# First stage of an encoder: x times rstd made ahead of the modulation for four half tiles, two of them reading the spread from PSUM

## The chip, the cores and the metric

The kernel runs on one core of one Trainium2 chip. The core has TensorE (PE, with its weight loads shown apart as PEld), VectorE (DVE), ScalarE (ACT), GpSimd (POOL) and SyncE (SP, which here issues the transfers). Each engine works through its own list of instructions in order, and waits at an instruction for what other engines or transfers must have done. The metric is the time of one execution on the device, in microseconds (us), lower is better.

## The reference

Two layers over 1024 tokens of 1024 channels. Each layer is conditioned by a vector c through a shift, a scale and a gate (adaLN); only the start of layer 0 matters here:

```python
def rms_norm(x, g):
    xf = x.astype(jnp.float32)
    y = xf * lax.rsqrt(jnp.mean(xf * xf, axis=-1, keepdims=True) + EPS)
    return (y * g.astype(jnp.float32)).astype(x.dtype)
...
    c_act = jax.nn.silu(c)
    for l in range(DEPTH):
        mod = c_act @ ada_w[l] + ada_b[l]
        shift, scale, gate = jnp.split(mod, 3, axis=-1)
        h = rms_norm(x, norm_g[l]) * (1.0 + scale[:, None, :]) + shift[:, None, :]
        if l % 2 == 0:
            y = even_mixer(h, ...)      # proj = h @ w_in, then attention and a recurrence
        else:
            y = odd_mixer(h, ...)       # proj = h @ w_in, then neighbourhood attention
        x = x + gate[:, None, :] * y
    return rms_norm(x, final_g)
```

So every element of h is x · rstd(token) · gain(channel) + shift(channel), where rstd is one over the root of a token's mean square, and gain is norm_g · (1 + scale). Layer 0's first projection multiplies h by w_in.

## The kernel before, in words

x is kept transposed: channels on the 128 partitions, tokens along the free axis. It is eight tiles of 128 channels by 1024 tokens (xT, tiles 0 to 7), and each has two halves of 512 tokens (half 0 and half 1). A pair of tiles, 2g and 2g+1, is a group g.

A product in fp32 quality is made from three products in a shorter format: high by high, high by low and low by high. Weights come as slabs of 128 output channels, 128x1024 with all eight tiles of input channels (raw). ScalarE rounds a slab to its high part (whi, L185), GpSimd subtracts to get its low part (wlo, L186). For the activations ScalarE writes the high part (ahi, L408) and VectorE the low one (alo, L409).

The first stage runs while x, the first slabs and the pieces of the adaLN weights (ada) are still coming in:

- `squares(hf, on_dve, ...)` loads the eight tiles of a half and squares them, some on VectorE (L528: tiles 2 and 5 in half 0; 1, 4 and 7 in half 1) and the others on ScalarE (L530). PE adds the squares up over the channels (L371, 32 matmuls of 128 columns for a half, of which the profile lists 64 passes, into a bank of PSUM named norm). In half 1 tile 7 is the first that is added, and the others follow it.
- `scale(hf)`: eleven small operations on VectorE make rstd of 512 tokens, folded to 128x128 (`rstd_rows`, L381 to L387), PE spreads it to all partitions (L400, into the same bank), and ScalarE copies that from PSUM to SBUF (bcs, L548).
- `mod_first(g)`: PE makes shift and scale of group g from ada and c (L276), ScalarE copies the row (mrow, L299), PE turns it into columns (L301), and VectorE makes shift (first, L305) and gain (L307).
- `parts(g, hf)` calls `make_h` for the two tiles: on VectorE x becomes x · gain · bcs (L407), ScalarE adds the shift for the high part (L408), VectorE makes the low part (L409). The tile is overwritten by x · rstd · gain, to which a later stage adds the shift again.
- `products(i, g, hf)`: the three products of slab i with each of the two tiles (L566, L567, L568), added up in PSUM banks, one for each of slabs 0, 1, 2 and half.

The kernel is written in a rough order, and a scheduler sets the order of each engine's list from that order, its estimates of times, and two marks: `tc.high_priority()` (the block is taken early) and `tc.issue_after(x)` (not before instruction x has been taken). The list of each engine is fixed when the kernel is built. SP's list of transfers is one of these.

Behind the first stage come the rest of layer 0's projections, differential attention, the recurrence, the output projection, and layer 1. They are not touched.

## Time and profile before

| | before |
|---|---|
| runs of the kernel, us | 1191.19, 1193.62, 1196.17 |
| median, us | 1193.62 |
| profiled execution, us | 1190.94 |
| its span in the profile, us | 1189.2 |
| mean granted clock of TensorE | 0.994 |
| share of the span busy: PE, PEld, DVE, ACT, POOL | 96%, 82%, 62%, 47%, 31% |

The span runs from the first to the last instruction that the profile has; the profiled execution's own time is 1.7 us longer. Rows of a timeline read: start in us, length in us (of the whole row, where several instructions follow each other as one row, xN), engine, line, operation, what it writes and reads, and in brackets how long the engine had been idle before it and who released it. A row of a group with three numbers in a line (476/482/2407) gives the shortest, the middle and the longest of its instructions in ns.

### The profile page before, as it was taken

Reading aid. Unit: us, or ns where it says so; the run is one execution under the profiler, and the core shown is the slowest. Engines: PE = TensorE matmul, PEld = TensorE weight load, DVE = VectorE, ACT = ScalarE, POOL = GpSimd, SP = SyncE. Lnnn points to the kernel's source line nnn. Section 1 sums busy time; section 2 is a strip of 40 time slices with the busy share of each in tenths; the row PEclk is TensorE's granted clock in tenths of the full one; section 3 lists DMA queues with packets and bytes.
Section 4 is the critical chain, followed back from the end, with each engine's and each line's share of the span. In section 5 each row is a group of like instructions: output and inputs, shape, how many; then the busy total and the mean of one; then the engine's idle time right before and its main releaser. Section 6 shows DMA issues by size and latency. Waiting matters only on the chain.

```text
span 1189.2 us, 19214 instructions
## 1 busy us (share of the span) xinstructions
PE 1142.0 (96%) x7232; PEld 972.3 (82%) x7232; DVE 735.6 (62%) x1422; ACT 564.4 (47%) x1029; POOL 372.5 (31%) x346
## 2 busy tenths in 40 slices
PE   4999899999998999999999999999999999999997
PEld 3788668888887888777878888988998998888896
DVE  6867948699889989768763334233434443556354
ACT  4358486465655556523443444344444434445121
POOL 2124321243333322344413333332333333326100
PEclk8999999999999999999999999999999999999999
DMA  9723132422123112476513442243453544314212
GB/s 331 234 87 117 53 96 74 141 74 82 37 79 88 32 39 72 136 245 225 181 53 121 136 116 83 87 141 101 131 171 96 152 133 120 90 38 161 92 72 71
DMA packets 85789, 136.46 MB, mean 115 GB/s; under 512 B 8000, under 2 KB 49472, under 8 KB 85696
## 3 DMA queue, kind: packets, MB, share of 16 engines
q1 hardware_dynamic: 85696, 135.23, 36.4%
q8 instruction: 57, 0.93, 0.3%
q14 instruction: 36, 0.29, 0.1%
HBM read 112.13 MB, written 16.78 MB: 108 GB/s over the span
## 4 chain that ended last, share of the span: by engine, by line
PE 75%; DVE 12%; ACT 5%; DMA 3%; issue 2%; POOL 2%; SPq 0%; DVEq 0%; ACTq 0%; POOLq 0%
PE pp L201 14%; PE pp L203 14%; PE pp L202 14%; PE no L1383 4%; PE etr L1365 3%; PE v L201 2%; PE v L203 2%; PE v L202 2%; PE n L662 2%; PE atr L998 2%; DVE e L968 2%; PE n L663 2%; PE s L662 1%; PE s L663 1%; POOL wlo L186 1%
## 5 line engine op out<-in xcount | busy, mean ns | idle before, releaser
L201 PE MATMUL pp<-ahi,whi 128*128 128x512 f32 (+1 forms) x976 | 370.2, 379 | 1.0 <-DVE sgb L668 0.9
L203 PE MATMUL pp<-ahi,wlo 128*128 128x512 f32 (+1 forms) x976 | 367.7, 377 | 1.1 <-POOL wlo L186 1.1
L202 PE MATMUL pp<-alo,whi 128*128 128x512 f32 (+1 forms) x976 | 368.0, 377 | 0.0
L186 POOL TENSOR_TENSOR wlo<-raw,whi 128x1024 fp32r<-128x1024 f32 x80 | 196.8, 2463 | 267.6 <-ACT whi L185 249.1
L203 PEld LDWEIGHTS pp<-ahi,wlo 128*128 128x128 f32 x976 | 183.8, 188 | 35.4 <-POOL wlo L186 1.6
L201 PEld LDWEIGHTS pp<-ahi,whi 128*128 128x128 f32 x976 | 183.8, 188 | 34.0 <-DVE sgb L668 1.7
L202 PEld LDWEIGHTS pp<-alo,whi 128*128 128x128 f32 x976 | 183.9, 188 | 30.4
L1354 POOL TENSOR_SCALAR e<-e,r 128x288 f32<-128x288 f32 (+1 forms) x128 | 71.5, 572 | 234.7 <-DVE r L1352 234.4
L185 ACT ACTIVATE whi<-raw 128x1024 fp32r<-128x1024 f32 x80 | 84.3, 1056 | 105.3 <-PE pp L202 57.4
L972 ACT ACTIVATE e<-e,nm 128x1024 f32<-128x1024 f32 x64 | 73.6, 1150 | 47.1 <-DVE nm L968 46.7
L1349 ACT ACTIVATE e<-e,nm 128x288 f32<-128x288 f32 (+1 forms) x128 | 72.7, 569 | 46.1 <-DVE nm L1346 39.3
L1371 DVE COPY e<-etr 96x384 f32<-96x384 f32 (+1 forms) x64 | 35.5, 555 | 94.3 <-PE etr L1365 92.7
L1346 DVE CUSTOM_DVE_ANT_0 e<-n,bias 128x288 f32<-128x288 f32 (+1 forms) x128 | 60.6, 505 | 46.9 <-PE n L663 32.9
L1369 ACT ACTIVATE e<-etr 96x384 f32<-96x384 f32 (+1 forms) x64 | 31.3, 490 | 118.2 <-DVE e L1371 116.7
L968 DVE CUSTOM_DVE_ANT_0 e<-s,tb 128x1024 f32<-128x1024 f32 x64 | 77.3, 1219 | 6.7 <-PE s L663 4.9
L989 POOL TENSOR_SCALAR e<-e,r 128x256 f32<-128x256 f32 x32 | 32.7, 1021 | 131.6 <-DVE r L978 81.4
L201 PE MATMUL v<-whi,ahi 128*128 128x256 f32 x256 | 72.2, 282 | 0.0
L203 PE MATMUL v<-whi,alo 128*128 128x256 f32 x256 | 71.9, 281 | 0.0
L202 PE MATMUL v<-wlo,ahi 128*128 128x256 f32 x256 | 71.9, 281 | 0.0
L1005 ACT ACTIVATE ath<-atr 128x512 fp32r<-128x512 f32 x64 | 37.5, 596 | 38.1 <-PE atr L998 37.8
L1365 PE MATMUL etr<-ident,e 128*96 128x128 f32 (+1 forms) x384 | 52.5, 272 | 2.0 <-POOL e L1354 2.0
L662 PE MATMUL s<-ks,qq 128*128 128x512 f32 x128 | 52.5, 410 | 0.4 <-DVE nm L968 0.4
(218 smaller groups left out, 2108.5 us busy)
## 6 DMA issues: line engine op xcount, KB each, us to landing
raw<-in_w_dram SPq DMA_DIRECT2D x56, 512.0 KB
ada<-in_adaw_dram SPq DMA_DIRECT2D x96, 256.0 KB
raw<-in_wo_dram SPq DMA_DIRECT2D x24, 512.0 KB
bias<-in_nab_dram SPq DMA_DIRECT2D x64, 144.0 KB
qq<-qq SPq DMA_DIRECT2D x48, 128.0 KB
bias<-in_nab_dram SPq DMA_DIRECT2D x32, 192.0 KB
xT<-in_xT_dram SPq DMA_DIRECT2D x16, 256.0 KB
vd<-vt SPq DMA_DIRECT2D x32, 128.0 KB
```

Of the source, the lines that this page charges most:

```text
L185: A.activation(hi[:], raw[:], AF.Copy)
L186: G.tensor_tensor(lo[:], raw[:], hi[:], ALU.subtract)
L201: T.matmul(ps, lh, rh, start=start, stop=False)
L202: T.matmul(ps, lh, rl, start=False, stop=False)
L203: state["pe"] = T.matmul(ps, ll, rh, start=False, stop=stop).ins
L662: T.matmul(dst, qsel(q[m]), k, start=True, stop=False)
L968: state["dve"] = V.tensor_tensor_reduce(out=e[:], in0=ps[:].rearrange("p a b -> p (a b)"), in1=tbt["tb"][:, o:o + S], scale=-1.0, scalar=3 ...
L972: A.activation(e[:], e[:], AF.Exp, scale=-1.0, bias=nm[:], accum_out=sums[:, m:m + 1])
L1346: state["dve"] = V.tensor_tensor_reduce(out=e[:, m, :n], in0=ps[:, m, :n], in1=bias["now"][m][:, :n], scale=-1.0, scalar=3.0e38, op0=ALU.a ...
L1349: A.activation(e[:, m, :n], e[:, m, :n], AF.Exp, scale=-1.0, bias=nm[:, m:m + 1], accum_out=sums[:, m:m + 1])
L1354: state["pool"] = G.tensor_scalar(e[:, m, :n], e[:, m, :n], r[:, m:m + 1], 0.0, ALU.mult, ALU.add).ins
L1365: T.transpose(pt[:kn, m, j * P:(j + 1) * P], e[:, m, j * kn:(j + 1) * kn], ident[:])
```

## The change

For tiles 0, 1, 2 and 3 of half 0 the product with rstd is an instruction of its own (`scale_x`, a TENSOR_TENSOR on VectorE), issued before the gain is known: for tiles 0 and 1 straight after the spread, reading it from its bank in PSUM (norm), for tiles 2 and 3 behind the low part of tile 1, reading bcs. `make_h` then, for these four, lets ScalarE multiply by the gain and add the shift in one instruction (a scale and a bias pointer), and after it VectorE multiplies the tile by the gain (TENSOR_SCALAR) and makes the low part as before. The other tiles of group 0 (0 and 1 in half 1) keep the fused product, and read norm where they read bcs.

```diff
-    def make_h(l, k, hf, x, bc):
+    def make_h(l, k, hf, x, bc, scaled=False):
...
-        V.scalar_tensor_tensor(x, x, g, bc, ALU.mult, ALU.mult)
-        A.activation(hi[:], x, AF.Identity, bias=b)
-        V.scalar_tensor_tensor(lo[:], x, b, hi[:], ALU.add, ALU.subtract)
+        if scaled:
+            A.activation(hi[:], x, AF.Identity, scale=g, bias=b)
+            V.tensor_scalar(x, x, g, None, ALU.mult)
+        else:
+            V.scalar_tensor_tensor(x, x, g, bc, ALU.mult, ALU.mult)
+            A.activation(hi[:], x, AF.Identity, bias=b)
+        state["lo"] = V.scalar_tensor_tensor(lo[:], x, b, hi[:], ALU.add, ALU.subtract).ins
         hact[k, hf] = (hi, lo)
...
+        scaled = set()
+
+        def scale_x(k, hf):
+
+            V.tensor_tensor(half(k, hf), half(k, hf), (bcs if k > 1 else nbank)[hf][:], ALU.mult)
+            scaled.add((k, hf))
+
         def parts(g, hf):
             for k in (2 * g, 2 * g + 1):
-                make_h(0, k, hf, half(k, hf), bcs[hf][:])
+
+                make_h(0, k, hf, half(k, hf), (bcs if g else nbank)[hf][:], (k, hf) in scaled)
...
         scale(0)
+        scale_x(0, 0)
+        scale_x(1, 0)
         parts(0, 0)
+        with tc.issue_after(state["lo"]):
+            scale_x(2, 0)
+            scale_x(3, 0)
```

In the changed kernel the lines shift: the multiplication is L558, the high part of a tile that is scaled already L408, its plain product L409, the fused product L411, the high part behind it L412, the low part L413, VectorE's square L532, ScalarE's L534, the copy of the spread L552. VectorE's list grows from 1395 to 1399 rows, the other lists keep their lengths. The lists of GpSimd and SP are the same as before; those of PE, VectorE and ScalarE differ within the first stage alone. In the rows below the numbers behind a name count buffers: xT_116 to xT_123 are tiles 0 to 7, ahi_0 and alo_0 belong to half 0, ahi_1 and alo_1 to half 1, raw_299 and raw_300 and so on to the slabs.

VectorE, from the end of rstd of half 0 to the first small operation for half 1, before:

```order
L305 TENSOR_TENSOR first_291<-mod_239,sm 128x4
L307 SCALAR_TENSOR_TENSOR gain_292<-first_291,sm 128x2
L407 SCALAR_TENSOR_TENSOR xT_116<-xT_116,gain_292,bcs 128x512
L407 SCALAR_TENSOR_TENSOR xT_117<-xT_117,gain_292,bcs 128x512
L409 SCALAR_TENSOR_TENSOR alo_0_322<-xT_116,first_291,ahi_0_321 128x512
L409 SCALAR_TENSOR_TENSOR alo_0_327<-xT_117,first_291,ahi_0_326 128x512
L528 TENSOR_TENSOR sq<-xT_117 128x512
L528 TENSOR_TENSOR sq<-xT_120 128x512
L528 TENSOR_TENSOR sq<-xT_123 128x512
L381 TENSOR_SCALAR rs<-norm_339 128x128
```

and in the changed kernel:

```order
L558 TENSOR_TENSOR xT_116<-xT_116,norm_190 128x512
L558 TENSOR_TENSOR xT_117<-xT_117,norm_190 128x512
L305 TENSOR_TENSOR first_291<-mod_239,sm 128x4
L307 SCALAR_TENSOR_TENSOR gain_292<-first_291,sm 128x2
L409 TENSOR_SCALAR xT_116<-xT_116,gain_292 128x512
L413 SCALAR_TENSOR_TENSOR alo_0_324<-xT_116,first_291,ahi_0_323 128x512
L532 TENSOR_TENSOR sq<-xT_117 128x512
L409 TENSOR_SCALAR xT_117<-xT_117,gain_292 128x512
L413 SCALAR_TENSOR_TENSOR alo_0_329<-xT_117,first_291,ahi_0_328 128x512
L558 TENSOR_TENSOR xT_118<-xT_118,bcs 128x512
L558 TENSOR_TENSOR xT_119<-xT_119,bcs 128x512
L532 TENSOR_TENSOR sq<-xT_120 128x512
```

Between the gain and the squares of tiles 4 and 7 stood two products, two low parts and the square of tile 1. Now there are two plain products, two low parts, the square of tile 1 and two multiplications there, and two multiplications stand ahead of L305; behind the last row shown, the square of tile 4, come that of tile 7 and L381.

ScalarE, from the copy of the spread of half 0 to the first of half 1's squares, before:

```order
L548 ACTIVATE bcs<-norm_190 128x512
L299 ACTIVATE mrow<-mod_239 128x128
L185 ACTIVATE whi_388<-raw_299 128x1024
L408 ACTIVATE ahi_0_321<-xT_116,first_291 128x512
L408 ACTIVATE ahi_0_326<-xT_117,first_291 128x512
L530 ACTIVATE sq<-xT_116 128x512
```

and in the changed kernel:

```order
L552 ACTIVATE bcs<-norm_190 128x512
L299 ACTIVATE mrow<-mod_239 128x128
L408 ACTIVATE ahi_0_323<-xT_116,first_291,gain_292 128x512
L185 ACTIVATE whi_392<-raw_299 128x1024
L408 ACTIVATE ahi_0_328<-xT_117,first_291,gain_292 128x512
L534 ACTIVATE sq<-xT_116 128x512
```

The first high part stands ahead of the second slab's high part (L185) where it stood behind it. GpSimd's low part of that slab (L186) waits for this L185.

VectorE behind the gain of group 1, which follows the second spread, before:

```order
L305 TENSOR_TENSOR first_446<-mod_394,sm 128x4
L307 SCALAR_TENSOR_TENSOR gain_447<-first_446,sm 128x2
L407 SCALAR_TENSOR_TENSOR xT_118<-xT_118,gain_447,bcs 128x512
L407 SCALAR_TENSOR_TENSOR xT_116<-xT_116,gain_292,bcs 128x512
L407 SCALAR_TENSOR_TENSOR xT_117<-xT_117,gain_292,bcs 128x512
L409 SCALAR_TENSOR_TENSOR alo_0_626<-xT_118,first_446,ahi_0_625 128x512
L409 SCALAR_TENSOR_TENSOR alo_1_491<-xT_116,first_291,ahi_1_490 128x512
L409 SCALAR_TENSOR_TENSOR alo_1_496<-xT_117,first_291,ahi_1_495 128x512
L407 SCALAR_TENSOR_TENSOR xT_119<-xT_119,gain_447,bcs 128x512
L407 SCALAR_TENSOR_TENSOR xT_118<-xT_118,gain_447,bcs 128x512
```

and in the changed kernel:

```order
L305 TENSOR_TENSOR first_450<-mod_398,sm 128x4
L307 SCALAR_TENSOR_TENSOR gain_451<-first_450,sm 128x2
L411 SCALAR_TENSOR_TENSOR xT_116<-xT_116,gain_292,norm_343 128x512
L411 SCALAR_TENSOR_TENSOR xT_117<-xT_117,gain_292,norm_343 128x512
L409 TENSOR_SCALAR xT_118<-xT_118,gain_451 128x512
L409 TENSOR_SCALAR xT_119<-xT_119,gain_451 128x512
L413 SCALAR_TENSOR_TENSOR alo_1_495<-xT_116,first_291,ahi_1_494 128x512
L413 SCALAR_TENSOR_TENSOR alo_1_500<-xT_117,first_291,ahi_1_499 128x512
L413 SCALAR_TENSOR_TENSOR alo_0_630<-xT_118,first_450,ahi_0_629 128x512
L413 SCALAR_TENSOR_TENSOR alo_0_635<-xT_119,first_450,ahi_0_634 128x512
```

The fused products of tiles 0 and 1 of half 1 come first now and read norm; the product of tile 2 was first before. On ScalarE the copy of the spread stands ahead of all high parts in both kernels.

## The prediction

> **What bounds the kernel now.** First the page's totals beside the busy times of two stretches: where is TensorE short of work?
>
> ```profile
> PE 1142.0 (96%) x7232; PEld 972.3 (82%) x7232; DVE 735.6 (62%) x1422; ACT 564.4 (47%) x1029; POOL 372.5 (31%) x346
> ```
>
> ```profile
> 0.00:40.00 40.00, 22.93 (x299) 16.50 (x300) 26.95 (x89) 16.36 (x27) 9.47 (x13) 0.91 1.00 338
> 40.00:130.00 90.00, 89.89 (x521) 73.37 (x520) 68.04 (x77) 59.47 (x82) 26.10 (x13) 1.00 0.33 110
> ```
>
> The columns behind the length are busy PE, PEld, DVE, ACT and POOL, the granted clock, the DMA share and GB/s. From 40 us on PE is busy for 89.89 of 90 us; in the first 40 us, where the change lies, for 22.93. Once PE is dense nothing waits that the change touches, so **a shift of the point where PE becomes dense goes whole into the end**. That point is the first product after the second spread, at 38.63 in the order in time of PE:
>
> ```profile
> 22.79 0.50 PE L566 MATMUL start<-ahi,whi 128*128 128x512 f32 x1 [1.99 <-ACT ahi L408]
> ...
> 29.18 2.55 PE L371 MATMUL norm<-sq,ones 128*32 128x128 f32 x64
> 31.66 0.50 PE L566 MATMUL start<-ahi,whi 128*128 128x512 f32 x1
> ...
> 33.25 1.95 PE L276 MATMUL mod<-ada,c 128*32 128x128 f32 x64
> 35.35 1.16 PE L400 MATMUL norm<-rr,sel 128*128 128x128 f32 x8 [0.15 <-DVE rr L387]
> 36.35 0.28 PE L301 MATMUL mod<-pick,mrow 128*128 128x4 f32 x2
> 38.63 0.50 PE L566 MATMUL start<-ahi,whi 128*128 128x512 f32 x1 [1.99 <-ACT ahi L408]
> ```
>
> Two waits of 1.99 us for a high part are what the diff can shorten. Between them stands a chain: sums of squares (29.18 to 31.73), eleven small VectorE steps, the second spread (35.35). The next two views are VectorE and ScalarE in the same stretch.
>
> ```profile
> 20.83 0.16 DVE L305 TENSOR_TENSOR first<-mod,sm 128x4 f32<-128x4 f32 x1 [2.89 <-PE mod L301]
> 21.03 0.16 DVE L307 SCALAR_TENSOR_TENSOR gain<-first,sm 128x2 f32<-128x2 f32 x1
> 21.23 3.52 DVE L407 SCALAR_TENSOR_TENSOR xT<-xT,gain,bcs 128x512 f32<-128x512 f32 x2
> 24.67 1.62 DVE L409 SCALAR_TENSOR_TENSOR alo<-xT,first,ahi 128x512 fp32r<-128x512 f32 x2
> 26.20 1.89 DVE L528 TENSOR_TENSOR sq<-xT 128x512 f32<-128x512 f32 x3
> 31.81 0.29 DVE L381 TENSOR_SCALAR rs<-norm 128x128 f32<-128x128 f32 x1 [3.71 <-PE norm L371]
> ```
>
> ```profile
> 19.26 0.60 ACT L548 ACTIVATE bcs<-norm 128x512 f32<-128x512 f32 x1 [7.11 <-PE norm L400]
> 20.08 0.28 ACT L299 ACTIVATE mrow<-mod 128x128 f32<-128x128 f32 x1 [0.22 <-PE mod L276]
> 20.26 1.05 ACT L185 ACTIVATE whi<-raw 128x1024 fp32r<-128x1024 f32 x1
> 22.02 0.72 ACT L408 ACTIVATE ahi<-xT,first 128x512 fp32r<-128x512 f32 x1 [0.71 <-DVE xT L407]
> 24.78 0.72 ACT L408 ACTIVATE ahi<-xT,first 128x512 fp32r<-128x512 f32 x1 [2.04 <-DVE xT L407]
> 25.41 2.69 ACT L530 ACTIVATE sq<-xT 128x512 f32<-128x512 f32 x5
> 28.01 1.04 ACT L185 ACTIVATE whi<-raw 128x1024 fp32r<-128x1024 f32 x1
> ```
>
> The two products of L407 took 3.52 us, although the two low parts of L409 behind them, as large and with as many inputs, took 1.62. Their rows have to be held against GpSimd's:
>
> ```profile
> 21.39 2.82 POOL L186 TENSOR_TENSOR wlo<-raw,whi 128x1024 fp32r<-128x1024 f32 x1 [11.97 <-ACT whi L185]
> 29.12 2.36 POOL L186 TENSOR_TENSOR wlo<-raw,whi 128x1024 fp32r<-128x1024 f32 x1 [4.92 <-ACT whi L185]
> ```
>
> ```profile
> 127.60 2.27 DVE L785 TENSOR_TENSOR_SCAN w<-t,t 128x1024 f32<-128x1024 f32 x1
> 129.78 3.35 DVE L780 TENSOR_TENSOR t<-t,w 128x1024 f32<-128x1024 f32 x1
> 133.06 1.21 DVE L787 TENSOR_TENSOR t<-t,w 128x1024 f32<-128x1024 f32 x1
> ```
>
> ```profile
> 128.23 3.82 POOL L186 TENSOR_TENSOR wlo<-raw,whi 128x1024 fp32r<-128x1024 f32 x1 [8.09 <-ACT whi L185]
> ```
>
> GpSimd's piece that came at 128.23, in the middle of a scan, first sat out the scan (to 129.87, then its 2.2 us); VectorE's next operation with two inputs in SBUF took 3.35 in place of the 1.21 of the one behind it, and ended 1.1 us after the piece. At 21.39 it is the same: the piece came during the first product, ended at 24.21, and both products were through at 24.75. So **the two engines take turns, GpSimd's waiting piece goes first, and VectorE loses 2.4 us and about 0.5 more**. The piece at 29.12 costs nothing, since VectorE is idle from 28.09 to 31.81.
>
> [...]
>
> **The change, part by part.** It adds four multiplications on VectorE, turns four fused products into plain ones, gives four high parts a scale pointer, and lets six operations read PSUM in place of the copy. Prices:
>
> ```profile
> L337 DVE TENSOR_SCALAR macc<-ada,ctmp x8: 476/482/2407, 81.0 to 930.5; 128x512 f32<-128x512 f32 x8
> ```
>
> ```profile
> L702 ACT ACTIVATE xc<-xb,sm x2: 1246/1246/1246, 65.9 to 69.2; 128x1024 f32<-128x1024 f32 x2
> ```
>
> A plain product by a pointer is 0.48 us (L337), a multiplication 0.69 (a square in L528 is of the same kind: three in 1.89, spaced 0.60, so the first takes 0.69). For the scale pointer there is no bare pair: L702 with two pointers took 1.25, L185 with none and as many elements 1.05, so one lies between nothing and 0.20 us; I take 0.10, and 0.82 for a high part. A fused operation with its second input in PSUM takes 0.68:
>
> ```profile
> L668 DVE SCALAR_TENSOR_TENSOR sgb<-sgb,pp x8: 662/678/691, 142.6 to 216.8; 128x512 f32<-128x512 f32 x8
> ```
>
> so PSUM or SBUF makes no price of its own here.
>
> *First half.* The first multiplication reads the spread in PSUM, but it waits for ScalarE's copy all the same (the program's wait; the copy reads that bank too). So it starts at 19.26 + 0.60, about 19.89, and the pair ends at 21.18. GpSimd is idle then, and nobody waits. L305 and L307, at 20.83 before, come behind it and end at 21.46 (0.27 late); the high part needs no product and runs 21.51 to 22.33; PE's first product starts at 22.38: **−0.41**. That is the wanted part, and the first bank of products is late for the rest anyway.
>
> *What moves with it.* ScalarE now puts the first high part ahead of whi of slab 1, which therefore runs 22.26 to 23.30 in place of 20.26 to 21.31. GpSimd hears of it at 23.37, in the low part of tile 0 (22.89 to 23.63), and takes its turn 23.63 to 25.99. Behind stand the square of tile 1, its plain product, its low part: 26.49, 26.90, 27.67 (the low part ended at 26.29 before). Then the multiplication of tile 2, 27.59 to 28.27. ScalarE, whose second high part no longer waits 2.04 us, ends its five squares at 26.62, and whi of slab 2 can run from then to 28.01, its time before: its GpSimd piece comes between 27.7 and 29.1. Before, VectorE was idle under that piece; now it has the multiplication of tile 3 and two squares to do, 28.27 to 30.2. Wherever in that stretch the piece falls before the last of them starts (29.5), it holds what is left for 2.36 + 0.5: **the square of tile 7 ends at 32.3, 4.2 us after 28.09**. Of this 1.4 are the two multiplications, 2.8 the second turn. Slab 1's products wait for its low part to 25.99 instead of 24.21, which the sums' later start covers. Its piece also frees a load's buffer 1.8 us later; the DMA engines are full all the while (share 1.00 to 40 us) and the orders on SP and GpSimd are as before, so I give that nothing; if a load were 1.8 late that the mod sums of 33.25 need, they would still come before the spread's 39.7.
>
> *Who waits.* PE's sums start with the square of tile 7 (the code adds it first) and all of PE's queue stands behind: sums at 32.4 in place of 29.18, **+3.2**, after some 3.5 us of idling. From there the clock decides:
>
> ```profile
> 20.20:23.63 3.43, 1.23 (x5) 0.78 (x5) 2.73 (x4) 1.82 (x3) 2.25 (x1) 1.00 1.06 392
> 23.63:27.05 3.42, 2.52 (x6) 1.59 (x6) 3.29 (x5) 2.27 (x5) 0.57 (x1) 0.50 1.06 366
> 27.05:30.46 3.41, 3.41 (x31) 2.38 (x33) 1.04 (x2) 2.00 (x4) 1.34 (x1) 0.50 1.11 350
> 30.46:33.87 3.41, 3.41 (x76) 2.67 (x70) 1.86 (x7) 0.00 (x0) 1.02 (x1) 1.00 1.07 370
> ```
>
> PE was granted half speed (0.50) for two stretches of 3.41 us, after one with 1.23 us of work; a stretch with 2.52 did not lift it, a full one did. So the sums ran 1.28 us at half and 1.27 at full speed, in 2.55; at full speed they would take about the 1.95 of the 64 passes in L276, so at half 1.88 times that, 3.67. With the gap before 32.4 neither 27.05 to 30.46 nor 30.46 to 33.87 is full, and half speed lasts to 37.28. Sums 32.4 to 36.07, then the 3.62 us of small steps (31.73 to 35.35) to 39.69. PE has six products meanwhile (1.59 us at full speed, 31.66 to 33.25: to about 38.0, three of them at half) and L276's 1.95: 39.95, then the spread. **+4.6.** Were the clock full throughout, sums end at 34.35 and the spread is at 37.97: **+2.6**. I take half speed, since the trace shows it after less idling.
>
> *Second half.* ScalarE's rows behind the spread:
>
> ```profile
> 36.55 0.60 ACT L548 ACTIVATE bcs<-norm 128x512 f32<-128x512 f32 x1 [1.01 <-PE norm L400]
> 37.85 2.05 ACT L408 ACTIVATE ahi<-xT,first 128x512 fp32r<-128x512 f32 x3 [0.70 <-DVE xT L407]
> ```
>
> The high part of tile 2 needs only its pointers, so the 1.99 us of waiting shrink: copy (0.60, now first) and high part instead of product and high part, about −0.7. But only two products hang on it. The next need the high part of tile 0, second half, which is product and then high part as before, and whose product waits for the copy as well: it comes 3.9 us after the spread in both. **0.** Adding up: +4.6 on the profiled execution, 1190.94, gives 1195.5. That execution is 2.7 under the median of 1193.62, so beside the runs **1198 us**, with 1196 (full clock) to 1199 as the likeliest case's own range (an L276 with half speed to its middle adds 0.7).
>
> [...]
>
> **Rivals.**
> 1. *The second GpSimd piece finds no victim or yields.* Then the square of tile 7 ends at 30.2, sums start there: at full clock +0.5, with half speed to 33.87 +2.0. 1194 to 1196. For it: the piece comes only 1.5 us before the point where it would cost nothing. Against: no row shows a waiting piece being passed.
> 2. *It does what the words say.* No collision reaches the sums, which start at 28.8, and half speed ends as before: −0.4; if PE, fed 0.4 us earlier, leaves half speed one stretch earlier, half of 3.41, −2.1 at most. 1191.5 to 1193. Against: six operations ahead of the square of tile 7 where four stood.
> 3. *The slower end: half speed one stretch longer.* If 33.87 to 37.28 is not full (a gap between sums and products would do), PE runs products (3.0) and L276 (3.67) at half: the spread at 36.07 + 6.67 = 42.7, +7.4, 1201. It decides from any gap of PE behind 33.87. Against: six products are ready there.
> 4. *The reading of PSUM skips no copy* is in my sum; if it did skip it, 0.6 us would be gained at the first spread (20.83 binds there, so nothing) and 0.6 at the second, on top of any case.
>
> **How the numbers follow.** The forecast 0.58, the first rival 0.14, the second 0.10, the third 0.18. About 0.5% (6 us, up to 1199.6) is what a measurement tells from no change. The forecast and the first two rivals stay inside it, but the runs of before lie up to 2.5 us from their own median, and the upper end of the forecast is 0.6 below the bound: 0.05 of its 0.58 falls beyond it. Slower then 0.18 + 0.05, about 0.23; faster needs −6 us, which no term here can give: 0.03; same 0.74. The range reaches from the second rival's middle, 1192, to the third's, 1201.5.
>
> **What would show it.** Right: PE's first product near 22.4; a GpSimd piece of 2.4 us with VectorE at tile 1's square, and a second one in the multiplication of tile 3; the square of tile 7 near 32.3 and the sums right behind it; a granted clock of 0.50 after 30.46; the spread near 40. Wrong: sums at 30 or earlier with VectorE unheld under the second piece, clock back at 1.00 at 30.46, or PE gaps behind 40 us, which would mean that a later stage pays or gains too.

## The result, and the profile after

The changed kernel takes 1199.89 us (median of 6 runs, 1198.52 to 1201.88) against 1193.57 of the kernel before (6 runs, 1191.19 to 1196.17): **1.0053 times as long, 95% interval 1.0036 to 1.0070**. In a second set, on another occasion, it was 1199.56 against 1192.67, ratio 1.0060 (1.0042 to 1.0078). So it is slower, by 6.3 and 6.9 us. That is just beyond the 0.5% (6 us) which the prediction took for what can't be told from no change, so on the side to which it gave 0.23; the intervals reach to both sides of that bound. The profiled execution is the longest of its six, 1201.88 us with a span of 1200.2.

VectorE in the changed kernel, in order of time:

```profile
20.67 1.28 DVE L558 TENSOR_TENSOR xT<-xT,norm 128x512 f32<-128x512 f32 x2 [2.86 <-ACT bcs L552]
...
24.70 2.88 DVE L532 TENSOR_TENSOR sq<-xT 128x512 f32<-128x512 f32 x1
...
28.67 3.44 DVE L558 TENSOR_TENSOR xT<-xT,bcs 128x512 f32<-128x512 f32 x2
32.03 1.28 DVE L532 TENSOR_TENSOR sq<-xT 128x512 f32<-128x512 f32 x2
```

GpSimd in the same stretch:

```profile
24.50 2.52 POOL L186 TENSOR_TENSOR wlo<-raw,whi 128x1024 fp32r<-128x1024 f32 x1 [15.22 <-ACT whi L185]
28.75 2.81 POOL L186 TENSOR_TENSOR wlo<-raw,whi 128x1024 fp32r<-128x1024 f32 x1 [1.73 <-ACT whi L185]
```

An undisturbed pair of multiplications takes 1.28 (the first row; the pair waited for ScalarE's copy, which ends at 20.65, although it reads PSUM). The square of tile 1 took 2.88, the pair of tiles 2 and 3 took 3.44: each lies under one of GpSimd's two pieces. The square of tile 7 is through at 32.03 + 1.28 = 33.31, where it was at 28.09 before. PE shows who waited for it:

```profile
17.96 2.04 PE L400 MATMUL norm<-rr,sel 128*128 128x128 f32 x8 [1.38 <-DVE rr L387]
...
23.52 0.50 PE L578 MATMUL start<-ahi,whi 128*128 128x512 f32 x1 [1.30 <-ACT ahi L408]
...
33.37 3.64 PE L371 MATMUL norm<-sq,ones 128*32 128x128 f32 x64 [3.34 <-DVE sq L532]
...
41.24 1.16 PE L400 MATMUL norm<-rr,sel 128*128 128x128 f32 x8
...
43.81 0.50 PE L578 MATMUL start<-ahi,whi 128*128 128x512 f32 x1 [1.29 <-ACT ahi L408]
...
45.13 0.50 PE L578 MATMUL start<-ahi,whi 128*128 128x512 f32 x1 [0.58 <-ACT ahi L412]
```

PE waited 3.34 us for the square, then needed 3.64 for the sums that had taken 2.55. The waits that the diff shortens did shrink, from 1.99 to 1.30 (23.52) and to 1.29 (43.81), and a new one of 0.58 stands two products later. The same stretch in rows of 3.40 to 3.42 us, cut so that the granted clock is either 0.50 or 1.00 throughout a row (length, busy PE, PEld, DVE, ACT, POOL, granted clock, DMA share, GB/s):

```profile
25.15:28.56 3.41, 2.73 (x7) 1.66 (x6) 3.37 (x3) 3.41 (x6) 1.87 (x1) 0.50 1.10 351
28.56:31.98 3.42, 1.47 (x4) 0.50 (x2) 3.42 (x3) 0.11 (x1) 2.81 (x1) 0.50 1.09 364
31.98:35.39 3.41, 2.02 (x40) 1.88 (x44) 1.33 (x3) 0.00 (x0) 0.00 (x0) 0.50 1.09 356
35.39:38.80 3.41, 3.41 (x36) 2.58 (x29) 1.55 (x6) 0.00 (x0) 0.00 (x0) 0.50 0.90 283
38.80:42.20 3.40, 3.40 (x75) 2.84 (x74) 1.59 (x6) 0.28 (x1) 0.00 (x0) 1.00 0.26 77
42.20:45.60 3.40, 1.52 (x8) 0.96 (x8) 2.86 (x7) 3.17 (x5) 0.00 (x0) 1.00 0.90 259
45.60:49.00 3.40, 3.40 (x13) 2.17 (x15) 3.40 (x6) 0.48 (x2) 0.00 (x0) 0.50 1.05 363
```

Half speed (a granted clock of 0.50) lasts four stretches, 25.15 to 38.80, where it lasted two before. Three of them had gaps (2.73, 1.47 and 2.02 us of work); the fourth is full (3.41), and full speed follows it. Then comes the thin stretch behind the second spread, 42.20 to 45.60 with 1.52 us of work, and one more at half speed follows that. Where the first convolution of the next stage starts (L702 before, at 65.9), the loss is 7.4 us:

```profile
L719 ACT ACTIVATE xc<-xb,sm x2: 1246/1246/1246, 73.3 to 76.5; 128x1024 f32<-128x1024 f32 x2
```

So where the time came from can be read at three marks of these two profiles: the sums start 4.2 us late (29.18 to 33.37), the first product of tile 0 of half 1 is 5.84 late (39.29 to 45.13), the next stage 7.4. The last step, from 5.84 to 7.4, is not shown to be the change's own (see why the prediction was right, below). The rest of the 11 us between these two profiled executions lies far behind, where both kernels run the same program (see the last section).

### The profile page after: what moved, and what is told of

Read it like the earlier page. It is cut to its first block, busy times and chain, and to the rows that moved or that the text cites. A ratio compares the mean times of both kernels' runs of the same rounds, so it can differ in the third digit from the quotient of the medians.

```text
span 1200.2 us, 19218 instructions
## 1 busy us (share of the span) xinstructions
PE 1152.1 (96%) x7232; PEld 978.8 (82%) x7232; DVE 739.9 (62%) x1426; ACT 563.9 (47%) x1029; POOL 371.2 (31%) x346
## 4 chain that ended last, share of the span: by engine, by line
PE 75%; DVE 13%; ACT 5%; DMA 3%; issue 2%; POOL 2%; SPq 0%; DVEq 0%; ACTq 0%; POOLq 0%
PE pp L201 14%; PE pp L203 14%; PE pp L202 14%; PE no L1400 4%; PE etr L1382 3%; PE v L201 2%; PE v L203 2%; PE v L202 2%; PE n L679 2%; DVE e L985 2%; PE atr L1015 2%; PE n L680 2%; PE s L679 1%; PE s L680 1%; POOL wlo L186 1%
## 5 line engine op out<-in xcount | busy, mean ns | idle before, releaser
L186 POOL TENSOR_TENSOR wlo<-raw,whi 128x1024 fp32r<-128x1024 f32 x80 | 196.7, 2461 | 268.7 <-ACT whi L185 246.4
L185 ACT ACTIVATE whi<-raw 128x1024 fp32r<-128x1024 f32 x80 | 84.3, 1056 | 106.4 <-PE pp L202 58.3
```

The source lines that it names most:

```text
L185: A.activation(hi[:], raw[:], AF.Copy)
L186: G.tensor_tensor(lo[:], raw[:], hi[:], ALU.subtract)
```

## The experiments

**Three theories.** *Late square*: the loss comes from the square of tile 7 of half 1, which the sums wait for, because two multiplications and GpSimd's second piece now stand ahead of it on VectorE. *Late slab*: it comes from slab 1's high part, which now stands behind the first activation on ScalarE, so that slab 1's low part and products come late. *Clock*: it is made of half-speed stretches that fall by chance. The table has the runs' medians, the median of the kernel before on the same occasion, and the ratio of the two sets of runs, which is not simply the quotient of the medians. Behind it are marks of each profile: the start of ScalarE's first copy of the spread, the end of the square of tile 7, the start of the sums, the start of the first product of tile 0 of half 1, and the start of the next stage's first convolution (L702 of the kernel before).

| kernel | median us (runs) | before, us | ratio, 95% interval | copy | square 7 | sums | product | next stage |
|---|---|---|---|---|---|---|---|---|
| before | 1193.57 (6) | 1193.57 | 1 | 19.26 | 28.09 | 29.18 | 39.29 | 65.9 |
| the change | 1199.89 (6) | 1193.57 | 1.0053, 1.0036 to 1.0070 | 20.05 | 33.31 | 33.37 | 45.13 | 73.3 |
| the change again | 1199.56 (6) | 1192.67 | 1.0060, 1.0042 to 1.0078 | 19.30 | 32.78 | 32.83 | 43.93 | 71.8 |
| change, squares 4 and 7 on ScalarE | 1194.18 (12) | 1193.29 | 1.0008, 0.9993 to 1.0022 | 19.48 | 27.80 | 28.99 | 39.29 | 67.6 |
| before, squares 4 and 7 on ScalarE | 1194.11 (12) | 1193.29 | 1.0010, 0.9999 to 1.0021 | 19.23 | 29.11 | 29.16 | 39.73 | 68.0 |
| change, squares ahead of multiplications | 1196.30 (12) | 1193.29 | 1.0022, 1.0008 to 1.0036 | 20.09 | 32.15 | 32.20 | 43.11 | 70.9 |
| only tiles 2 and 3 | 1194.52 (12) | 1193.29 | 1.0007, 0.9990 to 1.0024 | 20.25 | 31.13 | 31.73 | 41.19 | 69.4 |
| only tiles 0 and 1 | 1195.77 (12) | 1193.51 | 1.0025, 1.0008 to 1.0042 | 19.07 | 29.05 | 29.11 | 39.22 | 67.4 |
| change, GpSimd held | 1198.32 (9) | 1193.51 | 1.0040, 1.0022 to 1.0058 | 19.08 | 29.80 | 29.85 | 41.06 | 69.3 |
| change, PE's gap filled | 1197.32 (7) | 1193.51 | 1.0038, 1.0020 to 1.0057 | 20.13 | 33.47 | 33.52 | 42.98 | 69.8 |
| change, all from the copy | 1199.57 (6) | 1193.51 | 1.0060, 1.0045 to 1.0075 | 19.14 | 32.01 | 32.06 | 43.93 | 72.1 |
| squares ahead and GpSimd held | 1196.33 (12) | 1192.67 | 1.0031, 1.0014 to 1.0047 | 19.34 | 28.86 | 28.91 | 39.46 | 66.2 |
| the same again | 1193.46 (12) | 1193.74 | 1.0005, 0.9989 to 1.0022 | 20.22 | 30.16 | 30.22 | 40.78 | 67.5 |
| squares on ScalarE, more products | 1193.06 (12) | 1192.67 | 0.9999, 0.9986 to 1.0012 | 19.97 | 28.68 | 29.88 | 40.32 | 66.6 |

### The squares of tiles 4 and 7 on ScalarE

```diff
-            squares(1, (1, 4, 7), ptp, "pt")
+            squares(1, (1,), ptp, "pt")
```

> The whole change, with the squares of tiles 4 and 7 of half 1 on ScalarE in place of VectorE. Late-square theory (the loss comes from the square of tile 7, which the sums of half 1 wait for, standing behind two multiplications and GpSimd's second piece on VectorE): the sums start when PE's products end, near 30.0 us in place of 33.37, and half speed ends one stretch earlier, so 1195 to 1196 us, 4 to 5 less than the changed kernel. Late-slab theory (the loss comes from slab 1's high part standing behind the first activation on ScalarE, and its low part and products coming late): no gain, 1199 to 1201, since ScalarE's order up to there is unchanged. Clock theory (the loss is half-speed stretches that fall by chance): 1199 to 1200 on the mean of the runs.

1194.18 us, below the 1195 to 1196 expected: 5.7 less than the change, and not to be told from the kernel before. ScalarE and PE in this run:

```profile
24.07 3.73 ACT L534 ACTIVATE sq<-xT 128x512 f32<-128x512 f32 x7
```

```profile
28.99 2.30 PE L371 MATMUL norm<-sq,ones 128*32 128x128 f32 x64
...
37.97 0.50 PE L578 MATMUL start<-ahi,whi 128*128 128x512 f32 x1 [1.30 <-ACT ahi L408]
38.30 0.40 PE L579 MATMUL start<-ahi,wlo 128*128 128x512 f32 x1
39.29 0.50 PE L578 MATMUL start<-ahi,whi 128*128 128x512 f32 x1 [0.59 <-ACT ahi L412]
```

The sums start without a wait, at 28.99, and took 2.30. Slab 1's high part still stands behind the first activation (at 22.42 us in this profile, 20.26 before) and GpSimd starts its low part at 23.54 (21.39 before), and yet the loss is gone. So **late slab falls and late square stands**: what was moved is the sums' way alone. Half speed by chance, which had 1199 to 1200 here, falls too. The last three rows are the second finding. The first product behind the spread comes at 37.97 in place of 38.63, 0.66 earlier; the third comes at 39.29, to the hundredth where it stood before. The gain that the change is after reaches two products and stops.

The control, the kernel before with the same squares on ScalarE (the same line of the diff, applied there):

> The kernel before, with the squares of tiles 4 and 7 of half 1 on ScalarE: the control for the run beside it. Late-square theory: PE's products keep the sums at 29.2 us there, so nothing to gain, and ScalarE's two more squares of 0.55 us come before slab 2's high part, which is wanted only behind the sums: 1193 to 1194.5. A theory in which these squares on VectorE cost time of themselves: 1 to 3 us less than before, 1190.5 to 1192.5.

1194.11 us, 1.0010 of before: the squares' place costs or gains nothing of its own, as the first of the two expectations had it. The two runs beside each other, 1194.18 with the change and 1194.11 without, say that the change without its loss is worth nothing that can be measured.

### The multiplications behind the squares

```diff
-        with tc.issue_after(state["lo"]):
-            scale_x(2, 0)
-            scale_x(3, 0)
         with tc.issue_after(state["ada"].ins):
             squares(1, (1, 4, 7), ptp, "pt")
+        with tc.issue_after(state["sq"]):
+            scale_x(2, 0)
+            scale_x(3, 0)
```

(`state["sq"]` is the last square on VectorE.)

> The whole change, with the two multiplications of tiles 2 and 3 behind the square of tile 7 instead of ahead of the square of tile 4. Late-square theory in its two parts: 1.3 us of multiplications leave the way; GpSimd's second piece still comes while the square of tile 4 runs (28.7 us in the changed kernel's profile) and still holds the square of tile 7 up, to about 32.2 us in place of 33.3. So 1198 to 1199. If GpSimd's turn is not what holds it, the square of tile 7 is through at 30.0 and the time is 1195 to 1196. Late-slab theory: 1199 to 1201.

The square of tile 7 ended at 32.15, 0.05 from the 32.2 expected, since GpSimd's second piece now held the two squares. The time is 1196.30, less than the 1198 to 1199 expected; its profile shows half speed for three stretches where the change had four (single matmuls take 0.63 us from 25.43 on and 0.39 again from 35.86). Moving 1.3 us of multiplications out of the way is thus worth 1.2 us at the square (two profiles with the copy at 20.05 and 20.09) and 3.6 us between the medians; how much of that is the clock's chance isn't settled.

### Holding GpSimd back

```diff
             if hf:
+                hold = stp.tile([P, 1], F32, tag="hold", name="hold", bufs=1)
+                with tc.high_priority():
+                    G.tensor_tensor(hold[:], sqs[KC - 1][:, :1], sqs[KC - 1][:, :1], ALU.add)
                 ss_add(ss, sqs[KC - 1], True, False)
```

> The whole change, and GpSimd waits with slab 2's low part until the square of tile 7 of half 1 is through (a one-column addition that reads that square stands ahead of it on GpSimd; the computation is unchanged). VectorE's order is that of the change. Turn theory (GpSimd's second piece holds VectorE for 2.4 to 2.8 us): the square of tile 7 ends at 30.4 to 30.6 us in place of 33.31, the sums start right behind, and the piece itself then ends near 33, which the sums cover: 1195 to 1197. A theory in which VectorE's own added work makes it late: 33 us as before, and 1199 to 1201, or more, since slab 2's low part comes later.

VectorE, and then GpSimd, in this run (L561 is the multiplication here, L541 the added column):

```profile
27.31 1.28 DVE L561 TENSOR_TENSOR xT<-xT,bcs 128x512 f32<-128x512 f32 x2
28.51 1.29 DVE L532 TENSOR_TENSOR sq<-xT 128x512 f32<-128x512 f32 x2
```

```profile
29.88 0.19 POOL L541 TENSOR_TENSOR hold<-sq 128x1 f32<-128x1 f32 x1 [4.22 <-DVE sq L532]
30.02 2.36 POOL L186 TENSOR_TENSOR wlo<-raw,whi 128x1024 fp32r<-128x1024 f32 x1
```

In the same order on VectorE the pair of multiplications takes 1.28 in place of 3.44, and the square of tile 7 ends at 29.80 in place of 32.0 to 33.3. That **GpSimd's turn costs VectorE 2.2 us at this place is shown by taking the turn away**. At the end the gain is smaller than expected: 1198.32, outside 1195 to 1197, with runs from 1194.0 to 1199.55. In its profile PE still waited 1.19 us for the square, and the sums still took 3.64 us, as at half speed throughout. How much of the remaining 4.8 us over the kernel before is this and how much is chance, these runs don't settle.

### Filling PE's gap

```diff
             if hf:
+                for _ in range(7):
+                    ss_add(ss, sqs[KC - 2], True, True)
                 ss_add(ss, sqs[KC - 1], True, False)
```

> The whole change, and seven rounds of added matmuls (56 passes, about 3.2 us at half speed) on the square of tile 6, written to the bank of the sums and overwritten by them, in TensorE's gap ahead of the sums (29.9 to 33.4 us). They compute nothing that is used. If half speed is held by the gap: the stretch ahead of the sums is full, so TensorE is at full speed one or two stretches earlier, the sums take 1.95 us or little more in place of 3.64 and the products behind them are faster too; the sums start at most 0.3 us later: 1197 to 1198.5. If the clock doesn't depend on that gap: 1199.5 to 1201.

PE in this run, and its stretches of the clock:

```profile
30.10 2.79 PE L371 MATMUL norm<-sq,ones 128*32 128x128 f32 x56
33.52 1.96 PE L371 MATMUL norm<-sq,ones 128*32 128x128 f32 x64 [0.63 <-DVE sq L532]
```

```profile
28.80:32.20 3.40, 3.40 (x44) 2.46 (x46) 3.40 (x4) 0.01 (x1) 2.83 (x1) 0.50 1.08 368
32.20:35.60 3.40, 2.77 (x89) 2.28 (x81) 1.32 (x4) 0.00 (x0) 0.00 (x0) 0.98 1.10 352
```

The square of tile 7 is as late as in the change (33.47, 33.31 there), yet the sums take 1.96 us in place of 3.64: with idle time filled by work that nobody uses, the stretch up to 32.20 is full (3.40 of 3.40 us, granted 0.50) and full speed follows it (0.98). The next product is 2.15 us earlier than in the change (42.98 for 45.13), from the same start (copy at 20.13 and 20.05). The time, 1197.32, lies inside the 1197 to 1198.5 expected. So a part of the change's loss is **half speed that PE's waiting brought with it: 1.7 us in the sums alone**, between these two profiles.

### One pair at a time, and the reading of PSUM

Only tiles 0 and 1 (the two calls for tiles 2 and 3 left out):

> Only tiles 0 and 1 get their product with rstd ahead; tiles 2 and 3 are done as before. GpSimd's second piece still falls ahead of the square of tile 7, so by the theory of two engines taking turns it ends near 32.2 us, as in the run with the squares first (32.1), and the time is that run's, 1196 to 1197.5. If the ready products of tiles 2 and 3 are worth something behind the second spread, this run is 0.5 to 1 us above that one; if their multiplications alone made the loss, it comes down to 1193 to 1194.5.

1195.77, where the run with the squares first had 1196.30, and just below the 1196 to 1197.5 expected; but not by the way expected. VectorE's last two squares and GpSimd's second piece in this profile:

```profile
27.77 1.28 DVE L532 TENSOR_TENSOR sq<-xT 128x512 f32<-128x512 f32 x2
```

```profile
28.42 2.87 POOL L186 TENSOR_TENSOR wlo<-raw,whi 128x1024 fp32r<-128x1024 f32 x1 [2.30 <-ACT whi L185]
```

The second square starts at 28.37 (1.28 for two, the second 0.68 long), GpSimd's piece comes at 28.42, finds it running, sits it out to 29.05 and needs its 2.24 after that. Coming 0.05 us later than the square's start, it cost VectorE nothing. This is the first rival of the prediction, met in the execution profiled. Here the first product of tile 0 of half 1 stands at 39.22, as before (39.29), so this profile shows no loss in the first stage, and where the median's 2.3 us come from stays open. The runs reach from 1191.1 to 1200.3; a piece that falls now before and now behind that start would do this, but only one execution was seen, and other versions scatter as much.

Only tiles 2 and 3 (the other two calls left out, and bcs read as before):

> Only tiles 2 and 3 get their product with rstd ahead; tiles 0 and 1 are done as before, so slab 1's high part stands ahead of the first activation again. Late-square theory: GpSimd's first piece falls on the products as before, two multiplications push the square of tile 7 from 28.1 to 29.3 us, and GpSimd's second piece comes at 29.1, too late to hold it; the sums start 0.2 to 0.3 us late: 1193.5 to 1195. Late-slab theory: as the kernel before, 1193 to 1194. A theory that two multiplications cost by themselves what the change costs: 1197 or more. If the high part of tile 2 without a product brings what the change is after: 1192 to 1193.

1194.52, ratio 1.0007: inside the late-square range, and no gain from the ready products. The profile's square is later than expected (31.13 for 29.3), because in this execution shift and gain of group 0 came 1.85 us later than in the profile of before (22.68 for 20.83), and everything behind them; the piece at 30.95 came in the last square and held nothing.

All products from the copy in SBUF:

```diff
-            V.tensor_tensor(half(k, hf), half(k, hf), (bcs if k > 1 else nbank)[hf][:], ALU.mult)
+            V.tensor_tensor(half(k, hf), half(k, hf), bcs[hf][:], ALU.mult)
...
-                make_h(0, k, hf, half(k, hf), (bcs if g else nbank)[hf][:], (k, hf) in scaled)
+                make_h(0, k, hf, half(k, hf), bcs[hf][:], (k, hf) in scaled)
```

> The whole change with every product reading the copy in SBUF in place of PSUM. Since the reading of PSUM waits for the copy anyhow and takes as long, no difference: 1199 to 1201, first multiplication at the same time behind the copy. If PSUM's reading starts earlier or VectorE's reading of SBUF runs into GpSimd's piece: 1 to 2 us more than the changed kernel.

1199.57, as the change. The half of the change that reads PSUM does nothing here: the first pair of multiplications starts at 19.77, 0.03 behind the copy's end (19.14 + 0.60), and takes 1.29 us where it took 1.28 from PSUM. The change itself once more, on the occasion of the runs below:

> The change once more, beside the two runs that follow, since the runs scatter by some 5 us: 1199 to 1201. In its profile the square of tile 7 ends 2.5 to 3 us later than its own work needs, whatever the clock did at the start: near 32 us where the first spread's eight passes take 1.13 us, near 33.3 where they take 2.04.

1199.56. Here the first spread's eight passes took 1.13 us and not 2.04; the square of tile 7 ended at 32.78, between the two values expected, because the 24 passes of the modulation behind the spread took 1.51 in place of 0.86 us, and shift and gain came at 21.73:

```profile
18.14 1.13 PE L400 MATMUL norm<-rr,sel 128*128 128x128 f32 x8 [1.91 <-DVE rr L387]
...
40.03 1.16 PE L400 MATMUL norm<-rr,sel 128*128 128x128 f32 x8 [0.17 <-DVE rr L387]
...
43.93 0.79 PE L578 MATMUL start<-ahi,whi 128*128 128x512 f32 x1 [0.46 <-ACT ahi L412]
```

### Both cures on VectorE, twice

The multiplications behind the squares and GpSimd held, the two diffs above together:

> Both cures on VectorE at once: the multiplications of tiles 2 and 3 behind the square of tile 7, and GpSimd's second piece held until that square is through. Late-square theory: the square ends at 28.6 to 30 us (by the clock at the start), the sums start when TensorE's products end, and the time is that of the run with the squares on ScalarE, 1193 to 1195.5. GpSimd's piece then falls on the two multiplications, which nobody waits for. If something else in the change costs time (late slab, scale pointer, more instructions): above 1196.

The profile did what was expected (square at 28.86, sums at 28.91, product at 39.46), the time did not: 1196.33, its profiled execution 1198.44. So it was run again:

> The run with both cures on VectorE once more. Its profile showed the first stage cured (first product of tile 0 of half 1 at 39.46 us, 39.29 before), yet its time was 3 us above that. If its half-speed stretches behind 500 us fell there by chance, another set of executions gives 1193 to 1195.5; if the kernel itself brings them (or loses elsewhere), 1196 to 1197.5 again.

1193.46, ratio 1.0005, on another chip. The stretch from 500 to 700 us, which the change doesn't touch, in the first and the second of these profiles (of one kernel):

```profile
500.00:700.00 200.00, 193.38 (x1019) 162.13 (x1018) 114.89 (x187) 71.04 (x119) 70.17 (x46) 0.96 0.47 150
```

```profile
500.00:700.00 200.00, 194.02 (x1046) 162.34 (x1046) 117.45 (x193) 74.01 (x127) 71.35 (x48) 0.99 0.47 156
```

The granted clock differs by 0.03 over 200 us with the same program. By this the first set was a bad draw, as the expectation's first case had it, though two sets can't prove it: 12 runs each of one kernel lie 2.9 us apart, and their intervals hardly overlap. Differences of 2 to 3 us between single sets of the table (among the change with GpSimd held, with the gap filled, with the squares ahead) are therefore not settled by the times, only by the rows of their profiles; the 5 to 7 us between the change, in both its sets, and the cured kernels, in three sets of four, are: there the intervals lie apart.

### More products for the early high part

On top of the squares on ScalarE, group 1's parts of half 0 are made, and its products put, ahead of those of group 0 in half 1:

```diff
         parts(0, 1)
+        parts(1, 0)
...
+        for i in range(2):
+            products(i, 1, 0)
         for i in range(2):
             products(i, 0, 1)
...
-            for hf in range(2):
+            for hf in range(g == 1, 2):
                 parts(g, hf)
             for i in range(2):
-                for hf in range(2):
+                for hf in range(g == 1, 2):
                     products(i, g, hf)
```

> The change with the squares of tiles 4 and 7 on ScalarE, and the products of slab 1 with tile 2's high part put ahead of those of half 1, so that four products in place of two hang on the high part that comes early. If the gain behind the second spread is lost for want of products, the 0.59 us that TensorE waits for tile 0 of half 1 go down to 0.1 to 0.2, and 0.4 to 0.5 us less than with the squares on ScalarE alone, which only the profile can show: 1193 to 1194.5. If the gain was lost elsewhere, the wait stays.

```profile
39.00 0.50 PE L578 MATMUL start<-ahi,whi 128*128 128x512 f32 x1 [1.29 <-ACT ahi L408]
39.34 0.40 PE L579 MATMUL start<-ahi,wlo 128*128 128x512 f32 x1
39.57 0.40 PE L578 MATMUL start<-ahi,whi 128*128 128x512 f32 x1
39.80 0.40 PE L579 MATMUL start<-ahi,wlo 128*128 128x512 f32 x1
40.32 0.51 PE L578 MATMUL start<-ahi,whi 128*128 128x512 f32 x1
```

Four products run before tile 0 of half 1 is there, and PE's wait of 0.59 for it is gone: its first product starts 0.52 behind the start of the fourth, where it started 0.99 behind that of the second with the squares on ScalarE alone. The gain was lost for want of products that could use it, and can be had: 0.5 us of 1193, which the times (1193.06, ratio 0.9999, 0.9986 to 1.0012) can't tell from nothing. It is the fastest of the versions with the change in it, and no faster than the kernel before.

## Why the prediction was right, and where it missed

The forecast was that the change makes the kernel a little slower, by way of VectorE, GpSimd and the clock; measured are 6.3 us where 4.6 were forecast (on 1193.6), inside the range.

- *First product 0.41 earlier.* In the profile of the change it is 0.73 later (23.52), because the first spread's passes took 2.04 us there, in place of 1.13, and the copy began at 20.05. In the profiles that started as before did (copy at 19.08 and 19.14) the product comes at 22.16 and 22.23, 0.6 earlier, of which 0.1 to 0.2 is the copy's own earlier start. Right, and as was said, worth nothing at the end.
- *Slab 1's high part late, GpSimd's first piece on the square of tile 1.* Forecast to hold VectorE from 23.63 to 26.49, 2.86; it took 2.88.
- *GpSimd's second piece on the multiplication of tile 3.* By the prediction's times the pair runs from 27.59 to 31.13 (28.27, and 2.86 for the one that is held), 3.54; it took 3.44. The square of tile 7 was to end at 32.3: 33.31 in the late-starting execution, 32.01 and 32.78 in two others of the same order. Right, and shown by the run that took the turn away.
- *What a turn costs.* Here the prediction misread its rows. "2.4 us and about 0.5 more" is how long the held operation takes from start to end; its own 0.69 is in it. Lost are 2.2 (2.88 for 0.69, 3.44 for 1.28), and so too in its own rows (3.35 for 1.21). The 4.2 us of the square of tile 7 are then not 1.4 and 2.8: without the second turn its first rival has the square at 30.2, which is 2.1 late, and the turn adds the other 2.1. The sum is the same, since 32.3 was added up from the held operation's end.
- *Sums at half speed, 3.67 us.* 3.64, and half speed lasted four stretches, as forecast. The spread was to come at 39.95: 40.03 in two profiles, 41.24 in the late one.
- *No gain in the second half.* Right: with the squares on ScalarE the spread was at 35.39 and that product at 39.29, 3.90 behind it, where it was 3.94 before. In the change again, and with all from the copy, that product is 43.93, which is 4.64 later than before; the forecast's sum was 4.6. That the change again meets it so closely is in part luck: full speed was back there from 26.00 (a matmul takes 0.63 us at 25.38 and 0.39 at 26.87), and half speed returned just for the sums, behind the stretch in which PE waited for the square (last section).
- *Reading PSUM skips no copy.* Right: the first multiplication starts at 20.67, the copy ends at 20.65, and it was 1199.57 without PSUM. (By the diff four operations read PSUM, two multiplications and two fused products, not six; no term of the sum uses the number.)

**What missed, in both profiles of the change, is the step that the shift of the first product "goes whole into the end", with nothing added.** It goes into the end, but PE is not yet dense there. In the profile of the change it had 1.52 us of work in the stretch from 42.20 to 45.60, behind the spread, and got half speed for the next, 45.60 to 49.00, about 1.6 us more: from 5.84 late at the product to 7.4 at the next stage. In the second profile of the change it is 4.64 and then 5.9 (L719 at 71.8). The prediction's sum has no such term; its third rival (half speed one stretch longer) has one, ahead of the spread.

But this term is not shown to be the change's. By the table, 26.3 to 26.8 us lie between the product and the next stage in five profiles, that of before among them, and 27.8 to 28.3 in the nine others. The control and the change with the squares on ScalarE, both not to be told from the kernel before by their times, are among the nine. So the profile from which the prediction adds up had been spared a stretch that falls in either kernel (in the control's, matmuls take 0.63 us from 40.93 to 43.06; in that of before 0.39). Against the control's profile the change is 5.4 and 4.2 us late at the product, and 5.3 and 3.8 at the next stage: nothing is added. What makes 6.3 us of the 4.6 in the medians stays open; single profiles can't say whether the change meets such stretches more often.

The late-slab rival of the experiments never mattered: with the squares on ScalarE, PE's products ahead of the sums end at 29.0, no later than before (29.2), although slab 1's low part is late.

## What to carry to other kernels

Before work is put into an engine's idle time, look at what ends up behind it in that engine's queue and who waits for that: here 1.3 us of "free" multiplications stood ahead of the one square that all of TensorE waited for. Where two engines take turns, as VectorE and GpSimd did here (the pair of 1.28 us took 3.44 under GpSimd's piece), the idle time of the one may be the other's turn: what looked like a gap of 3.7 us on VectorE was the cover for GpSimd's piece of 2.36. And an operand made earlier is worth only as much as the work that can start with it; two products were too few.

## What was not expected of the hardware

- **The clock's stretches fall differently from profile to profile, and the same kernel moves by 7 us.** The 35 runs of the kernel before on one occasion reach from 1190.25, with a mean granted clock of 0.994, to 1197.30, with 0.985. The first spread's eight passes took 1.13 us in some profiles and 2.04 in others, with no difference in program ahead of them. Apart from the program's end, half speed came back once behind the first stage in the profile of before, near 529 us; in the profile of the change near 151, 537 and 650 us (the last for two stretches); in its second profile the granted clock from 500 to 700 us is 0.97, where it is 0.99 in that of before. As far as these profiles show, such stretches (four behind the first stage against one) are why the two profiled executions lie 11 us apart and the medians 6: the profile of before was a lucky one (2.7 under its median), that of the change an unlucky one (2 over).
- **A wait cost PE twice here.** With the gap filled by work thrown away, the same 64 passes took 1.96 in place of 3.64 us. In the second profile of the change half speed is seen to follow the wait: a stretch granted 1.00 with 0.00 us of work (the first row), then one granted 0.50, just that of the sums (the second). The rows from 39.65 are those behind its second spread:

```profile
29.41:32.82 3.41, 0.00 (x0) 0.00 (x0) 3.37 (x3) 0.00 (x0) 1.61 (x1) 1.00 1.08 368
32.82:36.24 3.42, 3.41 (x64) 2.96 (x64) 0.00 (x0) 0.00 (x0) 0.00 (x0) 0.50 1.10 352
...
39.65:43.06 3.41, 1.95 (x21) 1.49 (x12) 1.82 (x6) 2.11 (x4) 0.00 (x0) 1.00 0.81 257
43.06:46.48 3.42, 2.96 (x8) 2.07 (x7) 3.42 (x7) 1.43 (x3) 0.00 (x0) 0.50 1.02 323
```

- **How much work in a stretch keeps full speed is not one number here, as the profiles count work.** 1.92 us kept it in the first row of the kernel before that follows. In the second profile of the change 1.95 lost it (above), and in the first, whose rows come last, 1.78 lost it and 1.49 kept it. Nor does it take a full stretch to bring full speed back, as the prediction has it: a stretch with 2.85 us was followed by full speed in the kernel before (from 528.80), where one with 2.52 was not (from 23.63, in the prediction):

```profile
16.80:20.20 3.40, 1.92 (x32) 1.56 (x32) 1.04 (x4) 0.72 (x2) 0.00 (x0) 1.00 1.03 385
```

```profile
528.80:532.21 3.41, 2.85 (x7) 2.27 (x8) 2.71 (x3) 1.56 (x2) 2.89 (x2) 0.50 0.66 230
532.21:535.62 3.41, 3.41 (x17) 2.76 (x15) 0.52 (x1) 0.00 (x0) 0.00 (x0) 1.00 0.76 269
```

```profile
21.73:25.14 3.41, 1.78 (x6) 0.97 (x6) 2.15 (x6) 2.54 (x5) 0.64 (x1) 1.00 1.05 390
25.14:28.56 3.42, 2.74 (x7) 1.66 (x6) 3.38 (x3) 3.42 (x6) 1.88 (x1) 0.50 1.10 351
...
386.95:390.37 3.42, 1.49 (x7) 0.91 (x5) 3.32 (x6) 1.62 (x3) 2.82 (x2) 1.00 0.53 126
390.37:393.78 3.41, 3.35 (x21) 2.94 (x21) 3.31 (x8) 0.60 (x1) 2.40 (x3) 1.00 0.56 181
```

- **What GpSimd's turn cost VectorE went with the operation in which the piece came.** A piece that came 0.05 us behind the start of the last square held nothing and was held itself (2.87 for 2.24 of its own); one that came 0.08 behind the start of the square before that cost VectorE 2.2 us (the run with the squares ahead: 28.79 against 28.71). These are two versions of the kernel; no run moved the piece alone.
